# A fourth seven-product pair in every second gate and up group, and the sums of a paired slab one piece earlier

## The chip, the core and the metric

The kernel runs on one core of a Trainium2 chip. The metric is the device time of one execution in microseconds (us). The core has a matrix engine (TensorE, PE in the profile, with its weight loads shown apart as PEld), a vector engine (VectorE, DVE), a scalar engine (ScalarE, ACT), GpSimd (POOL) and SyncE (SP). In this kernel SP and POOL mostly issue DMA transfers, each from its own queue and in order.

## The reference: one layer of a hybrid encoder

256 rows of width 2048 go through an input projection into four mixers (gated linear attention, a Fourier mixer, long convolutions, a short convolution), an output projection, cross attention over 256 memory rows, and a gated feed-forward block, with a norm ahead of each and one at the end. Everything is fp32. The part that the change touches is the first half of the feed-forward block:

```
def swiglu(h, w_gate_up, w_down):
    gate, up = jnp.split(h @ w_gate_up, 2, axis=-1)
    return (jax.nn.silu(gate) * up) @ w_down
```

Here h is 256 x 2048, w_gate_up is 2048 x 11264 (5632 gate columns, then 5632 up columns) and w_down is 5632 x 2048.

## The kernel before

**Precision.** Every fp32 weight tile is split into a high part (a cast by ScalarE, `wh`) and the rest (a subtraction by VectorE, `wl`). Activations are kept split in the same way. One product of a 128 x 128 activation tile with a 128 x 512 weight tile is then three matmuls, in `part` (lines 433 to 435): high by `wh`, high by `wl`, low by `wh`. All three add into one PSUM bank.

**Slabs.** All weights are laid out in one array, in the order of use, as slabs of 128 x 2048 (four tiles of 128 x 512). `Stream` loads slabs (`_load`) into three `raw` buffers and splits them piece by piece into pairs `wh` and `wl`. There are four such pairs in these stages (three in one pool, a fourth in `extra`), used in turn, and `_fill` keeps at most four pieces in being: the one in use and three ahead. A plain slab (N in a plan) has two pieces of 1024 columns; it serves 8 products, 24 matmuls.

**Paired slabs.** For two k tiles, two column groups (512 gate columns and the 512 up columns that go with them) and the two halves of the 256 rows, eight products can be had from seven, if sums of weight tiles and sums of activation tiles are formed first. A paired slab (S in a plan) holds the four weight tiles and serves 7 products, 21 matmuls. The activation sums `z` are formed once by `combine`, before the first paired group. The weight sums are formed for each slab, in `_sums`, which makes four pieces of 1024, 512, 1024 and 1024 columns. They feed 2, 1, 2 and 2 products.

Weight sums come in two ways. For a slab in `SUMMED` (all paired slabs of gate and up) SP loads three of the four tiles, and two sums are made by a transfer: SP loads one tile twice into `two`, and a POOL transfer adds two others onto it (lines 99 to 103). VectorE then needs two additions. For the others (all paired slabs of the down projection) the whole slab is loaded and VectorE makes four additions, each of 512 columns. In both cases the additions are issued with the third piece (line 157), ahead of its cast (159) and subtraction (160).

**Groups.** Gate and up have 11 column groups. The first uses plain slabs only (`gemm_rows`). Each of the ten others is one call of `paired_rows` with the plan `GROUP`, eight slabs. After its last paired slab ScalarE and VectorE combine the sums (`mixed`, then `gated`); after its last slab `upped` finishes the gated product, VectorE transposes it and POOL stores it to DRAM (`store_turned`). POOL later loads it back, turned, and ScalarE and VectorE split it into the slots `f` of the down projection; this runs in the background.

**Order.** Each engine runs its instructions in the order in which they stand in the built program. That order comes from the order of the calls here and from a scheduler, which moves instructions by its own estimate. Background work (`Background`) is let in when a running count of VectorE work owed, `bg.dve(...)`, is small.

Of the kernel before, what the change touches and what calls it, by code (L numbers as in the profile page):

```python
# [13 lines left out]
F32 = mybir.dt.float32  # L14
F32R = mybir.dt.float32r
# [4 lines left out]
ALU = mybir.AluOpType  # L20
# [3 lines left out]
P = 128  # L24
# [3 lines left out]
DFF = 5632  # L28
# [13 lines left out]
LATE = 12  # L42

GATE_UP = 1920 // 16 + 8
GROUP = "NNSNSNSN"

DOWN = GATE_UP + 80
PASSES = "NNNNSNNSNNSNNSNNSNNSNN", "NSNSNSNSNSNSNSNSNSNNNN"

PAIRED = {a + i for a, plan in [(GATE_UP + 8 * j, GROUP) for j in range(10)] + [(DOWN, PASSES[0]), (DOWN + 22, PASSES[1])]  # L50
          for i, x in enumerate(plan) if x == "S"}
SUMMED = {i for i in PAIRED if i < DOWN}

LAG, OWED, SOON, FAR = 1.3, 0.9, 0.01, 18.0
V_NG = 0
# [16 lines left out]
class Stream:  # L72
# [21 lines left out]
    def _load(self, n):  # L94

        nc = self.nc
        self.raw = self.rawp.tile([P, 2048], F32, name="raw", tag="raw")
        if n // 16 + 1 in SUMMED:
            W, t = self.W[n // 16 + 1], self.sums.tile([P, 1024], F32, name="two", tag="two")
# [12 lines left out]
    def _half(self):  # L112

        nc, n = self.nc, self.made
        if n % 16 == 0 and self.phase == 0:
            self._load(n)
        if n // 16 in PAIRED:
            return self._sums()
# [21 lines left out]
    def _sums(self):  # L140

        nc, r, ph = self.nc, self.raw, self.phase
        summed = self.made // 16 in SUMMED
        if summed:
            src = (r[:, 512:1536], r[:, 0:512], self.two and self.two[0], r[:, 0:1024])[ph]
        else:
            src = (r[:, 512:1536], r[:, 0:512], r[:, 1024:2048], r[:, 0:1024])[ph]
        wh, wl = self._buffers(self.made, src.shape[1])
        if ph == 2:
            s = [r[:, i * 512:i * 512 + 512] for i in range(4)]  # L150
            if summed:
                t = self.two.pop(0)
                ops = ((s[1], t[:, 0:512], s[2]), (s[0], s[1], s[0]))
            else:
                ops = ((s[2], s[2], s[3]), (s[3], s[1], s[3]), (s[1], s[1], s[2]), (s[0], s[0], s[1]))
            for out, a, b in ops:
                nc.vector.tensor_tensor(out=out, in0=a, in1=b, op=ALU.add)  # L157
            self.bg.dve(512 * len(ops), len(ops))
        nc.scalar.copy(wh, src)  # L159
        nc.vector.tensor_tensor(out=wl, in0=src, in1=wh.bitcast(F32), op=ALU.subtract)  # L160
        self.bg.dve(src.shape[1])
        self.halves.append((wh, wl))
        self.phase = (ph + 1) % 4
        if ph == 3:
            self.made += 16
# [27 lines left out]
    def take_sums(self, w, ks, cols):  # L193

        assert self.n // 16 in PAIRED and self.n % 16 == 0
        self.order += [(w, ks[k], cols[c] + i * P) for k, c in ((1, 0), (0, 0), (1, 1), (0, 1)) for i in range(4)]
# [8 lines left out]
class Background:  # L205
# [17 lines left out]
    def first(self, g):  # L223

        self.q.sort(key=lambda e: e[0] is not g)
# [29 lines left out]
class Block:  # L255
# [208 lines left out]
    def paired_rows(self, w, cols, slots, sums, plan, mixed, first, ready=None, late=0, before=None, swap=False):  # L464

        st, s, nk = self.st, len(sums), len(slots)  # L470
        rest = [k for k in range(nk) if not any(k in ks for ks, _ in sums)]
        steps = [(c, k) for c in range(2) for k in rest]
        todo, q = iter(sums), {}
        count = {"a0": len(rest) + s, "a1": len(rest) + s, "b0": len(rest) + s, "b1": len(rest)}
        left, total = {}, 0

        def put(name, hi, lo, wh, wl):
            if name not in q:
                for x in [name] if name in count else "1675":
                    q[x] = (self.bank if (name in count) == swap else self.gbank)()  # L480
                    left[x] = count.get(x, s)
            new = left[name] == count.get(name, s)
            left[name] -= 1
            self.part(q[name][:, :], hi, lo, wh, wl, new, left[name] == 0)

        form = lambda t, r: (t[:, r * P:(r + 1) * P], t[:, R + r * P:R + (r + 1) * P])
        n = done = 0
        for i, kind in enumerate(plan):
            if before:
                before(i)  # L490
            if kind == "S":
                ks, z = next(todo)
                a = [form(slots[ks[0]], 0), form(slots[ks[1]], 0), form(slots[ks[1]], 1)]
                hi, lo, x4 = self.forms(z, slots[ks[0]])
                x1, s2, s3 = ((hi[:, i * P:i * P + P], lo[:, i * P:i * P + P]) for i in range(3))
                t = (("5", x1), ("7", s3))
                pairs = iter((("1", a[0]), ("b0", x4), ("a0", a[1]), *(t if st.n // 16 in SUMMED else t[::-1]), ("a1", a[2]), ("6", s2)))
                for parts in st.take_sums(w, ks, cols):
                    for wh, wl in parts:
                        name, (hi, lo) = next(pairs)  # L500
                        put(name, hi, lo, wh, wl)
                        self.bg.poll()
                done += 1
                if done == s:
                    mixed(*(q[i] for i in "1567"))
            else:
                for c, k in steps[n:n + 4]:
                    if ready:
                        ready(k)
                    wh, wl = st.take(w, k, cols[c], 4)  # L510
                    for r in range(2):
                        put("ab"[c] + str(r), *form(slots[k], r), wh, wl)
                        self.bg.poll()
                n += 4
            if first and done == s and n >= len(rest):
# [531 lines left out]
    def gate_up(self, gp, f, z):  # L1047

        nc = self.nc
# [7 lines left out]
        def up(j, ps, h=None):  # L1057
            h = h or [gp.tile([P, 512], F32, name="h", tag="h", bufs=2) for _ in range(2)]
            for r in range(2):
                self.stt(h[r], ps[r], box["col"][:, r:r + 1], g[r], ALU.mult, ALU.mult)  # L1060
                self.store_turned(self.ff, 4 * j, r, g[r], h[r])
            stored.append(self.bg.now)
# [16 lines left out]
        def upped(j, ps):  # L1079

            for r in range(2):
                self.tt(h[r], h[r], ps[r], ALU.add)
            up(j, h, h)
# [34 lines left out]
        def combined():  # L1118
            for ks, z in sums:
                yield 3.0  # L1120
                yield from self.combine(z, *(self.h3[k] for k in ks))

        sums = [((2 * i, 2 * i + 1), z[i]) for i in range(GROUP.count("S"))]
        comb = self.bg.add(combined())
        ps = self.gemm_rows("w_gate_up", [0, DFF], self.h3,
                            parts=[(range(8), [0]), (range(8, 12), [0]), (range(12), [1]), (range(12, 16), [0]), (range(12, 16), [1])],
# [4 lines left out]
        early = self.bg.add(fetch(0, FT - 22, 3, 2.0, 15))  # L1131
        self.bg.drain(comb)
        for j in range(1, DFF // 512):
            upped(j, self.paired_rows("w_gate_up", [j * 512, DFF + j * 512], self.h3, sums, GROUP, mixed, gated, swap=j % 2 == 0)[0])
        self.bg.drain(early)
        self.fetch = self.bg.add(fetch(FT - 22, FT, 6, SOON))

# [753 lines left out]
```

## Time and profile before

| | |
|---|---|
| median of 3 runs | 1437.34 us (1435.31, 1437.34 and one of 2798.02) |
| the profiled execution | 1435.07 us, of which the span of its instructions is 1433.3 us |
| PE busy | 1423.0 us, 99% of the span |
| VectorE busy | 1146.2 us, 80% |
| ScalarE busy | 815.2 us, 57% |
| the ten paired groups of gate and up | one each 41.48 us; the last runs to about 1193 us |
| DMA engines busy in one such group | 92 to 94%, 287 to 289 GB/s |

A page of the profile shows the busy time of each engine, then the span in 40 slices, the DMA queues, the chain of work that ended last, and the costliest groups of instructions. The time line gives start and duration of single instructions (or of a few equal ones, merged with their count), and in brackets how long the engine was idle before and what ended that. PE busy has one trap: a matmul is shown from its start to its modelled end, 0.39 us, while the next one starts 0.23 us after it. So the busy time of PE only says that no gap was left between matmuls.

### The profile page before, as it was taken

How to read it: one execution, taken by the hardware profiler on the slowest of the kernel's cores; microseconds unless marked ns; L12 is line 12 of the kernel's file. 1: busy time of each engine (PE TensorE's matmuls, PEld its weight loads, DVE VectorE, ACT ScalarE, POOL GpSimd, SP SyncE). 2: the span in 40 equal slices, each digit the busy share in tenths (PEclk: the TensorE clock that was granted, in tenths of full speed). 3: DMA queues.
4: the chain of work that ended last, by engine and by line, in shares of the span. 5: the costliest groups of instructions: out<-in, count | busy, mean ns of one | idle time of the engine just before them, and what ended most of it. 6: DMA issues, size and time to landing. Idle time of an engine off the chain costs nothing.

```text
span 1433.3 us, 18652 instructions
## 1 busy us (share of the span) xinstructions
PE 1423.0 (99%) x6589; PEld 1180.7 (82%) x6589; DVE 1146.2 (80%) x1738; ACT 815.2 (57%) x1183; POOL 234.8 (16%) x306
## 2 busy tenths in 40 slices
PE   9999999999999999999999999999999999999997
PEld 8888888888888888888888888888888888888886
DVE  6667868777877767777677888898888888989997
ACT  7556565446645555556554656555555556655655
POOL 0000100013212223531431121122011002000000
PEclk9999999999999999999999999999999999999999
DMA  9876564546667788964986999889999887655554
GB/s 352 299 285 248 205 206 162 175 169 224 202 196 236 234 267 252 274 200 166 289 239 209 286 286 277 278 275 282 294 293 288 268 260 229 219 230 179 193 218 147
DMA packets 73037, 343.79 MB, mean 240 GB/s; under 512 B 10957, under 2 KB 12654, under 8 KB 45168
## 3 DMA queue, kind: packets, MB, share of 16 engines
q1 hardware_dynamic: 54848, 288.98, 57.5%
q0 software_dynamic: 17664, 52.97, 15.8%
q8 instruction: 51, 0.84, 0.2%
q10 hardware_dynamic: 432, 0.66, 0.1%
q14 instruction: 42, 0.34, 0.1%
HBM read 322.12 MB, written 20.45 MB: 239 GB/s over the span
## 4 chain that ended last, share of the span: by engine, by line
PE 97%; DVE 1%; ACT 0%; DMA 0%; issue 0%; SPq 0%; ACTq 0%
PE pg L433 22%; PE pg L434 22%; PE pg L435 22%; PE pm L434 7%; PE pm L435 7%; PE pm L433 7%; PE pg L381 4%; PE pg L382 2%; PE pm L1344 1%; PE pm L1022 1%; PE pm L993 1%; DMA raw<-in_W 0%; PE pm L1753 0%; DVE res L283 0%; PE pm L994 0%
## 5 line engine op out<-in xcount | busy, mean ns | idle before, releaser
L136 DVE TENSOR_TENSOR wl<-raw,wh 128x1024 fp32r<-128x1024 f32 (+1 forms) x413 | 494.8, 1212 | 166.1 <-ACT wh L135 163.2
L135 ACT CAST wh<-raw 128x1024 fp32r<-128x1024 f32 (+1 forms) x413 | 424.5, 1043 | 283.9 <-PE pg L435 196.4
L433 PE MATMUL pg<-wh,act 128*128 128x512 f32 (+1 forms) x1191 | 465.6, 391 | 0.0
L434 PE MATMUL pg<-wl,act 128*128 128x512 f32 (+1 forms) x1191 | 463.9, 389 | 0.4 <-DVE wl L136 0.2
L435 PE MATMUL pg<-wh,act 128*128 128x512 f32 (+1 forms) x1191 | 463.9, 389 | 0.0
L433 PEld LDWEIGHTS pg<-wh,act 128*128 128x128 f32 x1191 | 223.8, 188 | 47.8 <-issue 1.5
L434 PEld LDWEIGHTS pg<-wl,act 128*128 128x128 f32 x1191 | 223.8, 188 | 47.2 <-DVE wl L136 1.3
L435 PEld LDWEIGHTS pg<-wh,act 128*128 128x128 f32 x1191 | 223.7, 188 | 47.2 <-DVE act L283 0.4
L159 ACT CAST wh<-raw 128x1024 fp32r<-128x1024 f32 (+1 forms) x150 | 137.0, 921 | 146.8 <-DVE raw L157 46.4
L160 DVE TENSOR_TENSOR wl<-raw,wh 128x1024 fp32r<-128x1024 f32 (+1 forms) x150 | 156.1, 1061 | 57.0 <-ACT wh L159 56.8
L434 PE MATMUL pm<-wl,act 128*128 128x512 f32 x309 | 120.5, 390 | 0.1
L433 PE MATMUL pm<-wh,act 128*128 128x512 f32 x309 | 120.2, 389 | 0.0
L435 PE MATMUL pm<-wh,act 128*128 128x512 f32 x309 | 120.2, 389 | 0.0
L381 PE MATMUL pg<-act,wh 128*128 128x512 f32 x256 | 90.5, 395 | 0.0
L382 PE MATMUL pg<-act,wl 128*128 128x256 f32 x256 | 71.8, 280 | 0.0
L434 PEld LDWEIGHTS pm<-wl,act 128*128 128x128 f32 x309 | 58.0, 188 | 13.0 <-DVE wl L136 0.6
L433 PEld LDWEIGHTS pm<-wh,act 128*128 128x128 f32 x309 | 58.0, 188 | 12.0
L435 PEld LDWEIGHTS pm<-wh,act 128*128 128x128 f32 x309 | 58.0, 188 | 12.0
L102 POOL DMA_DIRECT2D two<-in_W x30 | 26.6, 887 | 241.2 <-DMA two<-in_W 116.0
L157 DVE TENSOR_TENSOR raw<-raw 128x512 f32<-128x512 f32 x90 | 62.0, 689 | 1.3
L159 ACT CAST wh<-two 128x1024 fp32r<-128x1024 f32 x30 | 31.6, 1052 | 51.1 <-PE pg L435 21.7
L381 PEld LDWEIGHTS pg<-act,wh 128*128 128x128 f32 x256 | 48.1, 188 | 10.5
(375 smaller groups left out, 1821.9 us busy)
## 6 DMA issues: line engine op xcount, KB each, us to landing
raw<-in_W SPq DMA_DIRECT2D x216, 1024.0 KB, 5.6
raw<-in_W SPq DMA_DIRECT2D x30, 768.0 KB, 6.1
two<-in_W SPq DMA_DIRECT2D x60, 256.0 KB, 4.9
two<-in_W POOLq DMA_DIRECT2D x30, 512.0 KB, 9.3
raw<-in_W SPq DMA_DIRECT2D x11, 512.0 KB, 7.6
hidden<-g POOLq DMA_DIRECT2D x22, 256.0 KB, 3.7
tmp<-hidden POOLq DMA_DIRECT2D x44, 128.0 KB, 5.4
features<-tmp POOLq DMA_DIRECT2D x32, 128.0 KB, 5.3
```

The source lines that it names most:

```text
L102: nc.gpsimd.dma_start(t, W[:, 512:1536], accum_op=ALU.add)
L135: nc.scalar.copy(wh[:, a:b], r[:, a:b])
L136: nc.vector.tensor_tensor(out=wl[:, a:b], in0=r[:, a:b], in1=wh[:, a:b].bitcast(F32), op=ALU.subtract)
L157: nc.vector.tensor_tensor(out=out, in0=a, in1=b, op=ALU.add)
L159: nc.scalar.copy(wh, src)
L160: nc.vector.tensor_tensor(out=wl, in0=src, in1=wh.bitcast(F32), op=ALU.subtract)
L381: self.nc.tensor.matmul(p[:, :], wh, slot[:, :], start=start, stop=False)
L382: self.nc.tensor.matmul(p[:, 0:R], wl, slot[:, 0:R], start=False, stop=stop)
L433: self.nc.tensor.matmul(p, hi, wh, start=start, stop=False)
L434: self.nc.tensor.matmul(p, hi, wl, start=False, stop=False)
L435: self.nc.tensor.matmul(p, lo, wh, start=False, stop=stop)
L993: nc.tensor.matmul(p[:, :], q[d][:, r * P:(r + 1) * P], kt[d][:, :], start=d == 0, stop=False)
```

## The change

There are two edits.

**The sums move.** In `_sums` the additions are issued after the cast and subtraction of the second piece (`ph == 1`), no longer ahead of the third piece. For a summed slab the second addition now writes tile 2 instead of tile 0, so that the fourth piece is `r[:, 512:1536]` instead of `r[:, 0:1024]`; the last two products of such a slab swap places in `paired_rows`. Number and shape of the instructions of a slab stay the same.

**A fourth pair.** Groups 2, 4, 6, 8 and 10 get the plan `NSNSsNSN` instead of `NNSNSNSN`. Their slabs at places 1, 3 and 6 are summed slabs. The slab at place 4, marked s, is a paired slab that isn't in `SUMMED`: it is loaded whole, and VectorE makes its four sums. One more `z` tile holds the activation sums of the fourth pair of k tiles.

```diff
-GROUP = "NNSNSNSN"
+GROUPS = "NNSNSNSN", "NSNSsNSN"
...
-SUMMED = {i for i in PAIRED if i < DOWN}
+SUMMED = {GATE_UP + 8 * j + i for j in range(10) for i, x in enumerate(GROUPS[j % len(GROUPS)]) if x == "S"}
...
-        if summed:
-            src = (r[:, 512:1536], r[:, 0:512], self.two and self.two[0], r[:, 0:1024])[ph]
-        else:
-            src = (r[:, 512:1536], r[:, 0:512], r[:, 1024:2048], r[:, 0:1024])[ph]
+        t = self.two and self.two[0]
+        src = (r[:, 512:1536], r[:, 0:512], t if summed else r[:, 1024:2048], r[:, 512:1536] if summed else r[:, 0:1024])[ph]
         wh, wl = self._buffers(self.made, src.shape[1])
-        if ph == 2:
+        nc.scalar.copy(wh, src)
+        nc.vector.tensor_tensor(out=wl, in0=src, in1=wh.bitcast(F32), op=ALU.subtract)
+        self.bg.dve(src.shape[1])
+        self.halves.append((wh, wl))
+        if ph == 1:
             s = [r[:, i * 512:i * 512 + 512] for i in range(4)]
             if summed:
-                t = self.two.pop(0)
-                ops = ((s[1], t[:, 0:512], s[2]), (s[0], s[1], s[0]))
+                ops = ((s[1], t[:, 0:512], s[2]), (s[2], s[1], s[0]))
             else:
                 ops = ((s[2], s[2], s[3]), (s[3], s[1], s[3]), (s[1], s[1], s[2]), (s[0], s[0], s[1]))
             for out, a, b in ops:
                 nc.vector.tensor_tensor(out=out, in0=a, in1=b, op=ALU.add)
             self.bg.dve(512 * len(ops), len(ops))
-        nc.scalar.copy(wh, src)
-        nc.vector.tensor_tensor(out=wl, in0=src, in1=wh.bitcast(F32), op=ALU.subtract)
-        self.bg.dve(src.shape[1])
-        self.halves.append((wh, wl))
...
-            if kind == "S":
+            if kind in "Ss":
...
-                t = (("5", x1), ("7", s3))
-                pairs = iter((("1", a[0]), ("b0", x4), ("a0", a[1]), *(t if st.n // 16 in SUMMED else t[::-1]), ("a1", a[2]), ("6", s2)))
+                t, u = (("5", x1), ("7", s3)), (("6", s2), ("a1", a[2]))
+                back = slice(None, None, 1 if st.n // 16 in SUMMED else -1)
+                pairs = iter((("1", a[0]), ("b0", x4), ("a0", a[1]), *t[back], *u[back]))
...
-        sums = [((2 * i, 2 * i + 1), z[i]) for i in range(GROUP.count("S"))]
+        z = z + [gp.tile([P, 1024], F32R, name="z3")]
+        sums = [((2 * i, 2 * i + 1), z[i]) for i in range(4)]
...
-            upped(j, self.paired_rows("w_gate_up", [j * 512, DFF + j * 512], self.h3, sums, GROUP, mixed, gated, swap=j % 2 == 0)[0])
+            plan = GROUPS[(j - 1) % len(GROUPS)]
+            upped(j, self.paired_rows("w_gate_up", [j * 512, DFF + j * 512], self.h3, sums[:8 - plan.count("N")], plan, mixed, gated,
+                                      swap=j % 2 == 0)[0])
```

More of the change, by code (lines that the diff above doesn't have):

```diff
@@ L44 @@
 GATE_UP = 1920 // 16 + 8
-GROUP = "NNSNSNSN"
+GROUPS = "NNSNSNSN", "NSNSsNSN"
 DOWN = GATE_UP + 80
 PASSES = "NNNNSNNSNNSNNSNNSNNSNN", "NSNSNSNSNSNSNSNSNSNNNN"
-PAIRED = {a + i for a, plan in [(GATE_UP + 8 * j, GROUP) for j in range(10)] + [(DOWN, PASSES[0]), (DOWN + 22, PASSES[1])]
-          for i, x in enumerate(plan) if x == "S"}
-SUMMED = {i for i in PAIRED if i < DOWN}
+PAIRED = {a + i for a, plan in [(GATE_UP + 8 * j, GROUPS[j % len(GROUPS)]) for j in range(10)] + [(DOWN, PASSES[0]), (DOWN + 22, PASSES[1])]
+          for i, x in enumerate(plan) if x in "Ss"}
+SUMMED = {GATE_UP + 8 * j + i for j in range(10) for i, x in enumerate(GROUPS[j % len(GROUPS)]) if x == "S"}
 LAG, OWED, SOON, FAR = 1.3, 0.9, 0.01, 18.0
@@ L158, in _sums @@
             self.bg.dve(512 * len(ops), len(ops))
-        nc.scalar.copy(wh, src)
-        nc.vector.tensor_tensor(out=wl, in0=src, in1=wh.bitcast(F32), op=ALU.subtract)
-        self.bg.dve(src.shape[1])
-        self.halves.append((wh, wl))
+        if ph == 2 and summed:
+            self.two.pop(0)
         self.phase = (ph + 1) % 4
```

## The prediction

> **What bounds the kernel now.** I read the page's head and the chain of work that ended last, then busy time by stretch, then the waits, then the time line of one gate and up group.
>
> ```profile
> span 1433.3 us, 18652 instructions
> PE 97%; DVE 1%; ACT 0%; DMA 0%; issue 0%; SPq 0%; ACTq 0%
> ```
>
> ```profile
> 820.00:1235.00 415.00, 414.94 (x1829) 342.46 (x1828) 363.44 (x451) 236.92 (x288) 73.11 (x85) 1.00 0.89 274
> 1235.00:1400.00 165.00, 164.97 (x727) 135.83 (x726) 154.06 (x229) 96.25 (x127) 0.00 (x0) 1.00 0.55 203
> ...
> 944.10:985.58 41.48, 41.48 (x185) 34.35 (x183) 36.45 (x45) 24.19 (x30) 7.74 (x9) 1.00 0.92 289
> ...
> 1400.00:1433.00 33.00, 24.54 (x108) 19.55 (x106) 23.85 (x50) 15.86 (x29) 0.00 (x0) 0.94 0.45 159
> ```
>
> The columns are the stretch, its length, then busy time of PE, PEld, DVE, ACT and POOL, the granted clock, DMA share and GB/s. The chain is PE for 97%, and PE has no gap worth a name in gate and up (0.06 us in 415) or in the down projection (0.03 in 165). So time can be won only by taking matmuls away, and lost by any wait that reaches PE. The third row is one whole group: DVE works 36.45 of 41.48 us. It isn't far behind, so the waits need a look (all of 840 to 1200 us; total, times, longest):
>
> ```profile
> DVE wl L160 <- ACT wh L159: 41.7, 41, 1.7
> ACT wh L159 <- PE pm L435: 39.5, 28, 2.1
> ...
> PEld pm L434 <- DVE wl L160: 0.5, 1, 0.5
> ```
>
> PE's side waits once, for 0.5 us. ScalarE waits for PE, that is, for one of the four `wh`/`wl` pairs to come free: the supply is ahead by all that the pairs hold, and no more. How much that is in time depends on the slab.
>
> ```profile
> 933.90 0.39 PE L433 MATMUL pg<-wh,act 128*128 128x512 f32 x1
> ...
> 938.66 0.39 PE L433 MATMUL pm<-wh,act 128*128 128x512 f32 x1
> ...
> 944.10 0.39 PE L433 MATMUL pg<-wh,act 128*128 128x512 f32 x1
> ...
> 985.58 0.39 PE L433 MATMUL pm<-wh,act 128*128 128x512 f32 x1
> ```
>
> These are the starts of a paired slab (place 6), of the plain slab behind it, of the next group and of the one after. A paired slab takes 4.76 us for seven products, 0.68 each; a plain one 5.44 for eight. A plain piece therefore lasts PE 2.72 us, a paired piece 1.36, 0.68, 1.36 and 1.36. Over paired slabs the same four pairs hold half the time.
>
> **The change part by part.** *Matmuls.* Five groups swap a plain slab for a paired one: 5 products, 15 matmuls; the built program has 15 fewer. At 0.68 us each that is **-3.40 us**, certain, since PE has no gaps.
>
> *The fourth z.* Eight more small VectorE operations, once, of at most 0.42 us (row below), 3.4 us in all, and two casts. They fall into the first group, of plain slabs alone, where a slab asks 2.3 us of VectorE in 5.44. Cost nothing; without that cover 3.4 us.
>
> *The sums moved.* Down-projection slabs keep all their VectorE work; only small background operations change sides with the additions. PE waits 0.03 us there, so nothing can be gained; the pieces are ahead by more than the one or two background operations (0.42 us each) that change sides. I take 0, bounds 0 and +1 us.
>
> *Splits of the hidden tiles.* In the built order none of these stands in a changed group; those between hold four or five, and the last four stand together ahead of the down projection, whose first four slabs are plain. Cost 0.
>
> ```profile
> L283 DVE TENSOR_TENSOR f<-tmp,f 128x256 fp32r<-128x256 f32 x14 | 5.9, 419 | 0.0
> ```
>
> *The changed group.* I write T for time since the group's first matmul (944.10 in the trace). These rows carry the rest:
>
> ```profile
> 936.66 3.50 DVE L136 TENSOR_TENSOR wl<-raw,wh 128x1024 fp32r<-128x1024 f32 x3 [0.21 <-ACT wh L135]
> ...
> 944.66 1.22 DVE L136 TENSOR_TENSOR wl<-raw,wh 128x1024 fp32r<-128x1024 f32 x1 [0.38 <-ACT wh L135]
> 945.80 0.68 DVE L283 TENSOR_TENSOR g<-g,pm 128x512 f32<-128x512 f32 x1
> 946.40 1.28 DVE L283 TENSOR_TENSOR h<-h,pm 128x512 f32<-128x512 f32 x2
> 947.60 1.41 DVE L287 SCALAR_TENSOR_TENSOR h<-h,rc,g 128x512 f32<-128x512 f32 x2
> 948.92 1.30 DVE L557 STREAM_TRANSPOSE g<-h 128x512 f32<-128x512 f32 x2
> 950.14 1.18 DVE L136 TENSOR_TENSOR wl<-raw,wh 128x1024 fp32r<-128x1024 f32 x1
> 951.25 1.82 DVE L160 TENSOR_TENSOR wl<-raw,wh 128x1024 fp32r<-128x1024 f32 x2
> ...
> 955.05 0.69 DVE L157 TENSOR_TENSOR raw<-raw 128x512 f32<-128x512 f32 x1
> ```
>
> ```profile
> 1372.88 2.87 DVE L157 TENSOR_TENSOR raw<-raw 128x512 f32<-128x512 f32 x4
> 1375.66 1.22 DVE L160 TENSOR_TENSOR wl<-raw,wh 128x1024 fp32r<-128x1024 f32 x1
> ```
>
> ```profile
> 934.14 1.05 ACT L159 CAST wh<-raw 128x1024 fp32r<-128x1024 f32 x1 [1.71 <-PE pm L435]
> ...
> 1374.40 1.05 ACT L159 CAST wh<-raw 128x1024 fp32r<-128x1024 f32 x1 [2.64 <-DVE raw L157]
> ```
>
> A subtraction of 1024 columns takes 1.22 us and the next operation starts 1.14 after it (three in 3.50); one of 512 takes 0.69 and 0.60. Four additions hold VectorE 2.78 us (1372.88 to 1375.66), and a cast that needs two of them starts 1.52 us after the first (1374.40). A cast takes 1.05 and starts 0.24 us after PE frees its pair (933.90, where the plain slab ends, to 934.14). PE needs `wl` 0.23 us into a product. VectorE's work for the group: 36.45 less two plain subtractions (2.28), plus three of 1024, one of 512 and four additions (3.42 + 0.60 + 2.78) is 41.0 us, less 1.4 for four splits that go elsewhere: 39.6 of PE's 40.80. The mean just fits. The places where it doesn't are two.
>
> *Place 1.* From 944.66 (T+0.56) to 950.14 (T+6.04) VectorE does one subtraction and then the end of the last group. In the built order that subtraction is now the first piece of the paired slab; its second piece, the sums and the rest stand behind the block. VectorE's order there, in groups 4 and 8 of the changed program (its line 148 is the paired slab's subtraction, 158 its additions, 136 a plain slab's):
>
> ```
> L148 wl<-raw 1024     first piece, ahead of the block
> L282 g<-g  L282 h<-h x2  L286 h<-h x2  L557 g<-h x2
> L148 wl<-raw 512      second piece
> L158 raw<-two
> L148 wl<-two 1024     third piece
> L158 raw<-raw
> L136 wl<-raw 1024     slab behind, first piece
> L148 wl<-raw 1024     fourth piece
> ```
>
> In groups 2, 6 and 10 both pieces of the slab behind stand ahead of the fourth piece. PE used to have two plain slabs, 10.88 us, ahead of the first paired one; now it has 5.44.
> - VectorE: second piece T+6.04, done 6.73; addition at 6.64; third piece 7.24 to **8.46**; addition to 9.07; then, as built, one or two plain subtractions of the slab behind (8.99 to 10.21, or to 11.35), and the fourth piece to **11.48** or **12.49**.
> - PE: pieces begin at T+5.44, 6.80, 7.48. The third piece's `wl` is needed at 7.71: a wait of 0.75. It ends at 9.59; the fourth's `wl` is needed at 9.82: a wait of 1.66 where one plain subtraction stands ahead (groups 4 and 8), 2.67 where two do (2, 6, 10).
>
> Together 2.41 or 3.42 us. The lower bound is 0 (the order on the chip finds slack that I don't see), the upper 3.42 in all five groups.
>
> *Place 4, the slab s.* Its pieces follow those of a paired slab, whose pairs come free late in short steps. With t for PE's start on the paired slab at place 3: first pair free t+1.36, cast 1.60 to 2.65, subtractions 2.68 and 3.82, additions 4.42 to 7.29, third piece 7.20 to **8.42**. PE wants it at 4.76 + 2.04 + 0.23 = 7.03: a wait of 1.39, and that piece ends at 9.55. In the built order a plain subtraction stands ahead of the fourth piece as well: 8.34, then 9.48 to **10.70**, wanted at 9.78: 0.92. Together **2.31 us**. In the down projection the same additions hurt no one, since a plain slab (5.44 us) stands ahead of each such slab. Lower bound 0, if background order spares it; the upper bound comes with the load of the slab:
>
> ```profile
> raw<-in_W SPq DMA_DIRECT2D x38, 1024.0 KB, 7.5
> ```
>
> ```profile
> DMA to landing us min/median/max: 5.8/7.3/9.7
> ```
>
> SP can issue it when place 1's fourth piece is done (T+11.5 or 12.5), so it lands at about T+19.0 or 20.0, and its first cast is due at T+19.65 or 20.66. A load of 9.7 us would come 1.6 us late. I take 0; upper bound 1.6 in each of five groups. The added summed slabs' transfers (SP's, then POOL's) keep four slabs or more between the release of `two` and its next use, as now, and POOL's order has three of them per group as before: 0.
>
> *Sum.* Groups 4 and 8: 2.41 + 2.31 = 4.72; groups 2, 6 and 10: 5.73. Waits 2 x 4.72 + 3 x 5.73 = 26.6, less 3.4: **+23.2 us**. The profiled execution took 1435.07 us (its span and 1.8 around it), 2.3 below the median of the runs; from it 1458.3, and I say **1458 us**, 1.6% up. About 2% is what a measurement of this kernel can tell from no change.
>
> The Trainium skill (Perfetto Trace Analysis, Identifying the Most-Contended Engine) says that kernels generally improve when the most-contended engine is relieved; that is PE here, and by that rule the change gives the first rival's time. The 36.45 of 41.48 us that VectorE already works in a group, with a whole piece of lead lost at place 1, speaks against it.
>
> **The rivals.**
> - *Not slower: the four pairs cover it.* VectorE's mean work stays below PE's time, and the trace shows a lead of all four pairs almost always. If the third piece at place 1 is ready 0.75 us sooner and the slab s finds its first pairs 1.4 us sooner, no wait reaches PE: 1435.07 - 3.4 = **1431.7 us**. Against it: the block from 944.66 to 950.14 is fixed by PE's group end, and pairs aren't free before PE is done with them.
> - *Late load of s.* All five loads take 9.7 us: 5 x 1.6 = 8 more, **1466 us**, just over 2%. For it: DMA is busy 92% in a group; against it: the median leaves 0.65 us.
> - *The clock falls in the new gaps.* In the last 33 us PE stands 8.46 us idle and the clock is 0.94: 2.0 us lost, 0.23 for each idle us. On 26.6 us of gaps that is 6.3 more: **1465 us**. Against it: those end gaps are longer than mine, the longest of which is 2.67 us. The Trainium skill (TensorE: Matmul & The Clock Gate, HAM oscillation) puts the danger at idle gaps above about 3.4 us; by that rule the clock stays at 1.00 here. No run shown so far has such gaps in mid-kernel.
> - *It isn't done as said.* The built program has the four additions in five slabs and 15 matmuls fewer, so no.
>
> **How the numbers follow.** Forecast, waits at both places, 1444 to 1464: 0.68. Waits at one place alone or half as long, 1435 to 1444: 0.08. Not slower, about 1432: 0.08. Late loads, the clock, or waits that add up differently, 1464 to 1480: 0.16. The range 1438 to 1470 leaves out the not-slower rival, part of the half case and the far end of the last: near 0.2. Slower by over 2% (above about 1465): 0.17; faster by over 2%: 0.01, as no more than 3.4 us can be won; within: 0.82.
>
> **What would show it.** In the changed profile PE's idle time in the ten groups should be about 27 us, all in the five changed ones, ended by VectorE's `wl` of paired slabs; changed groups should last 45.5 and 46.5 us and the others 41.48 as now. At place 1 two gaps of 0.75 and 1.7 or 2.7 us, at place 4 of 1.4 and 0.9. Granted clock 1.00 and the down projection without gaps. The prediction is wrong if changed groups last 40.8 us, if their gaps end with a DMA, or if the other groups grow.

## The result, and the profile after

The changed kernel takes **1456.74 us** (median of four runs, 1456.05 to 1457.85), the kernel before 1437.09 on the same chip (median of four, one of which took 2798.02 us and is left out of the ratio): a ratio of **1.014 [1.0127, 1.0153]**, 1.4% slower. The forecast was 1458 us. The profiled execution took 1456.53 us (before: 1435.07), its span grew from 1433.3 to 1454.8, by 21.5 us.

The page's head, the busy time of each engine and the chain that ended last, of the kernel after:

```profile
span 1454.8 us, 18657 instructions
...
PE 1432.8 (98%) x6574; PEld 1176.6 (81%) x6574; DVE 1169.7 (80%) x1776; ACT 823.2 (57%) x1195; POOL 235.1 (16%) x306
...
PE 81%; DVE 9%; DMA 6%; ACT 2%; issue 2%; SPq 0%; ACTq 0%; DVEq 0%
```

VectorE's busy share is 80% as before; PE's share of the chain fell from 97 to 81%, VectorE's rose from 1 to 9, and that of the DMA, all of it loads of raw slabs, from 0 to 6. So the average didn't move, the order of what ends last did.

To see where, the span is cut at the first copy of each group's combining (`mixed`), which comes once per group. Busy time by stretch, kernel after: length, then PE, PEld, DVE, ACT, POOL, granted clock, DMA share, GB/s. These are groups 2, 3, 6 and 7:

```profile
810.15:857.01 46.86, 44.35 (x182) 34.59 (x181) 39.69 (x46) 24.34 (x29) 7.73 (x9) 0.96 0.88 260
857.01:898.45 41.44, 41.44 (x184) 34.26 (x183) 35.78 (x43) 24.28 (x30) 7.79 (x9) 1.00 0.89 273
985.59:1029.70 44.11, 42.55 (x181) 33.11 (x180) 39.99 (x48) 24.56 (x29) 6.06 (x7) 1.00 0.88 261
1029.70:1071.41 41.71, 41.71 (x185) 34.49 (x184) 36.02 (x43) 23.72 (x29) 6.06 (x7) 1.00 0.88 276
```

The full list is 46.86, 41.44, 45.28, 41.86, 44.11, 41.71, 43.89, 41.64 and 44.51 us; before, nine times about 41.48. A changed group without any wait would take 40.80 (41.48 less 0.68), so the five lose 6.1, 4.5, 3.3, 3.1 and 3.7 us, 20.7 in all; the groups between lose next to nothing. The first copy stands at 810.15 (before 810.17). From the last copy to the end it is 253.35 us, before 249.22: 4.1 more. So 20.7 in the changed groups, less 3.4 for the matmuls that went, plus 4.1 in the down projection, is 21.4 of the span's 21.5.

What PE waited for over the ten groups of the kernel after (total, times, longest):

```profile
PE pg L432 <- ACT wh L147: 4.6, 8, 1.0
PE pg L433 <- DVE wl L148: 4.0, 7, 0.7
PE pm L432 <- ACT wh L135: 0.9, 4, 0.2
```

Lines 147 and 148 are the cast and the subtraction of a paired slab. This view counts only idle time after a modelled end (0.39 us), so it shows less than is lost; from the starts of the matmuls, taken 0.23 us apart, the five groups lose 1.6, 2.1, 1.3, 2.1 and 1.9 us at **place 1** (9.1) and 2.4, 2.0, 1.9, 0.8 and 1.8 at **place 4** (9.0). Another 1.6 us of group 2 are a fallen clock (below). About 1 us of the 20.7 is in none of these sums.

Place 1 in group 6, VectorE's time line after:

```profile
1000.50 0.65 DVE L148 TENSOR_TENSOR wl<-raw,wh 128x512 fp32r<-128x512 f32 x1
1001.07 0.68 DVE L158 TENSOR_TENSOR raw<-two,raw 128x512 f32<-128x512 f32 x1
1001.66 1.22 DVE L148 TENSOR_TENSOR wl<-two,wh 128x1024 fp32r<-128x1024 f32 x1
1002.80 0.68 DVE L158 TENSOR_TENSOR raw<-raw 128x512 f32<-128x512 f32 x1
1003.40 2.35 DVE L136 TENSOR_TENSOR wl<-raw,wh 128x1024 fp32r<-128x1024 f32 x2
1005.67 2.35 DVE L148 TENSOR_TENSOR wl<-raw,wh 128x1024 fp32r<-128x1024 f32 x2
```

The second piece, an addition, the third piece, an addition, two plain pieces, the fourth piece: VectorE runs without a break behind the block of the last group, as the prediction wrote it down, and the fourth piece's `wl` is done at 1006.89. PE in the same stretch:

```profile
1002.43 0.50 PE L432 MATMUL pm<-wh,act 128*128 128x512 f32 x1
1002.93 0.50 PE L433 MATMUL pg<-wl,z 128*128 128x512 f32 x1
...
1004.62 0.49 PE L432 MATMUL pg<-wh,z 128*128 128x512 f32 x1 [0.48 <-ACT wh L147]
1004.95 0.39 PE L432 MATMUL pm<-wh,act 128*128 128x512 f32 x1
1005.18 0.40 PE L433 MATMUL pm<-wl,act 128*128 128x512 f32 x1
...
1007.26 0.39 PE L433 MATMUL pg<-wl,z 128*128 128x512 f32 x1
```

From 1004.95 to 1007.0 PE does three whole products of the plain slab *behind*, whose `wl` was done early, and only at 1007.26 turns to the fourth piece's `wl`. The gap is 0.65 us, where 2.67 were forecast, and it isn't a wait for `wl`. It ends with ScalarE's cast of the fourth piece, which starts when VectorE's second addition is done (1003.48):

```profile
1003.51 2.00 ACT L147 CAST wh<-raw 128x1024 fp32r<-128x1024 f32 x2 [0.19 <-DVE raw L158]
```

Place 4, the slab s. ScalarE's first two casts of s in groups 2, 4, 6 and 10, then that of its third piece in group 10:

```profile
839.30 1.57 ACT L147 CAST wh<-raw 128x1024 fp32r<-128x1024 f32 x2 [1.52 <-DMA raw<-in_W]
...
928.01 1.57 ACT L147 CAST wh<-raw 128x1024 fp32r<-128x1024 f32 x2 [1.30 <-DMA raw<-in_W]
...
1013.12 1.57 ACT L147 CAST wh<-raw 128x1024 fp32r<-128x1024 f32 x2 [0.54 <-DMA raw<-in_W]
...
1184.87 1.57 ACT L147 CAST wh<-raw 128x1024 fp32r<-128x1024 f32 x2 [0.35 <-PE pm L434]
1189.21 1.05 ACT L147 CAST wh<-raw 128x1024 fp32r<-128x1024 f32 x1 [2.78 <-DVE raw L158]
```

VectorE in group 10, the first two pieces of s, the additions and the third piece:

```profile
1185.95 1.83 DVE L148 TENSOR_TENSOR wl<-raw,wh 128x1024 fp32r<-128x1024 f32 x2 [0.18 <-ACT wh L147]
1187.69 2.86 DVE L158 TENSOR_TENSOR raw<-raw 128x512 f32<-128x512 f32 x4
1190.47 1.22 DVE L148 TENSOR_TENSOR wl<-raw,wh 128x1024 fp32r<-128x1024 f32 x1
```

So what comes last here is a chain: a pair or the load, a cast, two subtractions, the additions, the cast of the third piece, PE. In groups 8 and 10 the chain starts when PE frees a pair, as the prediction has it; in groups 2, 4 and 6 it starts with the load of s, 1.17, 1.17 and 0.18 us after the time at which the pair would have let the cast begin (in groups 8 and 10 it begins 0.47 us after the start of the last matmul that uses the pair). VectorE has pauses here: in group 10 it stops four times between 1180 and 1186, for 1.5 us in all, each time for a cast.

### The profile page after: what moved, and what is told of

Read it like the earlier page. It is cut to its first block, busy times and chain, and to the rows that moved or that the text cites. A ratio compares the mean times of both kernels' runs of the same rounds, so it can differ in the third digit from the quotient of the medians.

```text
span 1454.8 us, 18657 instructions
## 1 busy us (share of the span) xinstructions
PE 1432.8 (98%) x6574; PEld 1176.6 (81%) x6574; DVE 1169.7 (80%) x1776; ACT 823.2 (57%) x1195; POOL 235.1 (16%) x306
## 4 chain that ended last, share of the span: by engine, by line
PE 81%; DVE 9%; DMA 6%; ACT 2%; issue 2%; SPq 0%; ACTq 0%; DVEq 0%
PE pg L433 19%; PE pg L434 19%; PE pg L432 19%; DMA raw<-in_W 6%; PE pm L432 4%; PE pm L433 4%; PE pm L434 4%; PE pg L380 4%; DVE wl L136 3%; PE pg L381 2%; DVE wl L148 2%; DVE raw L158 1%; ACT wh L135 1%; PE pm L1347 1%; ACT wh L147 1%
## 5 line engine op out<-in xcount | busy, mean ns | idle before, releaser
L136 DVE TENSOR_TENSOR wl<-raw,wh 128x1024 fp32r<-128x1024 f32 (+1 forms) x403 | 483.3, 1212 | 164.2 <-ACT wh L135 161.9
L135 ACT CAST wh<-raw 128x1024 fp32r<-128x1024 f32 (+1 forms) x403 | 414.9, 1042 | 278.1 <-PE pg L434 192.6
L147 ACT CAST wh<-raw 128x1024 fp32r<-128x1024 f32 (+1 forms) x170 | 155.7, 922 | 169.3 <-PE pg L434 59.7
L148 DVE TENSOR_TENSOR wl<-raw,wh 128x1024 fp32r<-128x1024 f32 (+1 forms) x170 | 177.4, 1061 | 49.6 <-ACT wh L147 49.1
L432 PE MATMUL pm<-wh,act 128*128 128x512 f32 x279 | 109.4, 395 | 1.0 <-ACT wh L135 0.9
L433 PE MATMUL pm<-wl,act 128*128 128x512 f32 x279 | 109.6, 393 | 0.3 <-DVE wl L136 0.2
L434 PE MATMUL pm<-wh,act 128*128 128x512 f32 x279 | 108.9, 390 | 0.0
L158 DVE TENSOR_TENSOR raw<-raw 128x512 f32<-128x512 f32 x110 | 75.5, 687 | 1.6
L432 PEld LDWEIGHTS pm<-wh,act 128*128 128x128 f32 x279 | 52.5, 189 | 14.6 <-ACT wh L135 3.9
L433 PEld LDWEIGHTS pm<-wl,act 128*128 128x128 f32 x279 | 52.5, 188 | 13.8 <-DVE wl L148 1.7
L434 PEld LDWEIGHTS pm<-wh,act 128*128 128x128 f32 x279 | 52.5, 188 | 10.7
```

The costliest lines, as they stand in the source:

```text
L135: nc.scalar.copy(wh[:, a:b], r[:, a:b])
L136: nc.vector.tensor_tensor(out=wl[:, a:b], in0=r[:, a:b], in1=wh[:, a:b].bitcast(F32), op=ALU.subtract)
L432: self.nc.tensor.matmul(p, hi, wh, start=start, stop=False)
L433: self.nc.tensor.matmul(p, hi, wl, start=False, stop=False)
L434: self.nc.tensor.matmul(p, lo, wh, start=False, stop=stop)
```

## The experiments

Every kernel is the changed kernel with the edit shown. Periods are the stretches between first copies, as above; groups 2, 4, 6, 8 and 10 are the first, third, fifth, seventh and ninth.

### Each part alone

**The moved sums without the fourth pair.**

```diff
-GROUPS = "NNSNSNSN", "NSNSsNSN"
+GROUPS = "NNSNSNSN", "NNSNSNSN"
```

> The moved sums alone, all ten groups with the old plan. Theory A (the four weight pairs give too short a lead at places 1 and 4 of the changed groups, and the background work that they push back costs some 4 us at the start of the down projection): 1435 to 1438 us, no gap of PE in gate and up, none above 0.6 us at the start of the down projection. Rival B (the moved additions hold VectorE at the wrong moment, in either stage): 1445 us or more, or at least the 4 us at the start of the down projection.

Measured: 1436.74 us, 1.0002 [0.9993, 1.0012]; periods 41.5 to 41.7 but for the last (42.9), the last stretch 249.38. The busy time by stretch of this kernel, to be set beside the same stretch of before:

```profile
820.00:1235.00 415.00, 414.16 (x1822) 341.16 (x1821) 362.46 (x449) 236.53 (x287) 73.09 (x85) 1.00 0.89 273
```

PE is idle 0.84 us in 415, nearly all of it in the last period. The medians agree within the interval, so the move is worth nothing that these runs can tell.

**The fourth pair with the sums at the third piece, as they were.**

```diff
-        nc.scalar.copy(wh, src)
-        nc.vector.tensor_tensor(out=wl, in0=src, in1=wh.bitcast(F32), op=ALU.subtract)
...
-        if ph == 1:
+        if ph == 2:
...
                 nc.vector.tensor_tensor(out=out, in0=a, in1=b, op=ALU.add)
             self.bg.dve(512 * len(ops), len(ops))
+        nc.scalar.copy(wh, src)
+        nc.vector.tensor_tensor(out=wl, in0=src, in1=wh.bitcast(F32), op=ALU.subtract)
```

> The fourth pair alone, sums issued with the third piece as before. Theory A: 1454 to 1460 us, with gaps at the same two places and some 4 us at the start of the down projection. Rival B: 1434 to 1440 us. If the move helps the slab s at all, this one is slower than 1457 by some us.

Measured: 1456.38 us, 1.014 [1.0125, 1.0156], the same as the whole change. The fourth pair carries all of the loss; earlier sums neither caused it nor soften it. Its parts lie a little otherwise: the first copy 1.7 us later, the last stretch 250.91.

**A paired slab at place 1 alone**, three paired slabs, all summed by transfers:

```diff
+GROUPS = "NNSNSNSN", "NSNNSNSN"
```

> Changed groups with the plan NSNNSNSN: three summed pairs as before, only the first of them at place 1 in place of place 2; as many matmuls as before. Theory A: gaps of 1.3 to 2.3 us at place 1 in five groups as in the changed kernel, so some 9 us: 1443 to 1447 us. Rival C (only the slab s is at fault, by its four additions or its load): 1435 to 1438 us.

Measured: 1443.12 us, 1.0044 [1.0029, 1.0059]. The changed groups last 43.63, 42.86, 42.58, 42.60 and 42.59 against 41.48 (there are three paired slabs again, so no matmuls are saved): 6.9 us.

**The slab s behind a paired one alone**, with two plain slabs ahead, three paired slabs:

```diff
+GROUPS = "NNSNSNSN", "NNSsNNSN"
```

> Changed groups with the plan NNSsNNSN: three pairs, the second of them an s right behind the first; as many matmuls as before, place 1 plain. Theory A: gaps of 1.3 to 4.3 us behind the paired slab in five groups as in the changed kernel, some 12 us without place 1: 1445 to 1450 us. If place 1 were the only cause: 1435 to 1438 us.

Measured: 1442.64 us, 1.0043 [1.0026, 1.006], less than expected. The changed groups last 43.32, 42.83, 43.27, 43.33 and 42.74: 8.1 us over 41.48, and all gaps stand at the slab s. PE's waits in the groups of this kernel:

```profile
PE pg L432 <- ACT wh L147: 2.3, 5, 0.7
PE pm L432 <- ACT wh L135: 1.2, 5, 0.3
```

PE is held first by the cast of the slab's third piece, which waits for the additions. So the two places cost 13.5 us over before when each is alone (7.0 and 6.5 over the 1436.12 us that before took on that chip). The whole change loses 19.7, or 23.1 with its 3.4 us of saved matmuls: 9.6 come only with both together, of which 4.1 are the down projection and 1.6 the clock; the rest are longer waits at the two places (the slab s stands at place 3 here and at place 4 in the changed kernel, so the comparison is rough).

**The changed plan in groups 1, 3, 5, 7 and 9.** The two plans trade places:

```diff
+GROUPS = "NSNSsNSN", "NNSNSNSN"
```

> The changed plan in groups 1, 3, 5, 7 and 9 in place of 2, 4, 6, 8 and 10, so that a group of the old plan stands ahead of the down projection. Theory A (the changed kernel's 4.1 us in the down projection come from background work pushed back by the last groups): the down projection takes what it took before, and the whole 1451 to 1455 us. If that cost has another cause: 1456 to 1459 us.

Measured: 1455.75 us, 1.0126 [1.0108, 1.0144]; now the second, fourth, sixth and eighth periods are the long ones (44.75, 47.03, 46.01, 44.82) and the others are 41.3 to 42.2. The loss goes with the plan, not with where a group stands. The total lies between the two ranges: with a group of the old plan ahead of it, the last stretch falls by 2 us, to 251.3, and not to the 249.2 of before.

### Is it the pairs, or VectorE?

The prediction explained place 4 by pairs that come free late. A fifth pair should take that away; a kernel without the additions takes VectorE's work away.

**A fifth pair, with the plan NNSsNNSN, first with narrower pairs.** To make room the pairs became 1072 columns wide instead of 1088 (only 1024 are used).

```diff
+GROUPS = "NNSNSNSN", "NNSsNNSN"
...
-        return (pool.tile([P, 1088], F32R, name=t, tag=t)[:, at:at + m] for t in ("wh", "wl"))
+        return (pool.tile([P, 1072], F32R, name=t, tag=t)[:, at:at + m] for t in ("wh", "wl"))
...
+            pool = (self.wp, self.wp, self.wp, self.extra, self.fifth)[(i - self.h0) % 5]
```

> The plan NNSsNNSN of the run with s behind a paired slab (1442.6 us), with a fifth weight pair in use during the paired groups and so one piece more of lead (the four small tiles that it takes the room of come from the common pool). Theory A: the gaps behind the paired slab vanish or fall under 0.5 us: 1434 to 1438 us. If it is VectorE's throughput or the load of s that lacks and not the lead: 1441 us or more.

Measured: 1465.66 us, 1.0204 [1.0183, 1.0224]. It doesn't answer the question, since 13 us were lost *ahead* of the first paired group (first copy 823.45 instead of 810.2). The same holds for two runs with the same width, in which all four paired slabs were summed by transfers:

```diff
+GROUPS = "NNSNSNSN", "NSNSSNSN"
-tc.tile_pool(name="tw", bufs=2)
+tc.tile_pool(name="tw", bufs=3)
```

> The changed groups' slab s made a summed slab too (plan NSNSSNSN): two additions by VectorE in place of four, two more of its sums by a POOL transfer, with a third buffer for these. Theory A: the wait behind the paired slab falls from 1.3 to 4.3 us to under 1 us in five groups, that of place 1 stays: 1446 to 1452 us. Rival C (transfers late): no faster than the changed kernel, or gaps that end with a DMA.

```diff
+GROUPS = "NNSNSNSN", "NNSSNSSN"
-tc.tile_pool(name="tw", bufs=2)
+tc.tile_pool(name="tw", bufs=3)
```

> Changed groups with the plan NNSSNSSN, all four pairs summed, a third buffer for the sums: two plain slabs first, so no paired slab at place 1, and two additions in place of four behind a paired slab. As many matmuls as the changed kernel. Theory A: gaps under 1 us a group, and with 3.4 us of matmuls less 1432 to 1440 us. Rival C: each of these groups loads 0.75 MB more, and 1445 us or more with gaps that end with a DMA.

Measured: 1482.73 us, 1.0314 [1.0288, 1.034], and 1482.95 us, 1.0314 [1.0287, 1.0342], with first copies at 823.99 and 823.37. Two of the three were run again at 1088 columns.

**The fifth pair, pairs 1088 wide.** The edit is shown against the kernel with the narrower pairs.

```diff
-tile([P, 1072], F32R, name=t, tag=t)
+tile([P, 1088], F32R, name=t, tag=t)
```

> The plan NNSsNNSN of e4_behind in every second group, with a fifth wh/wl pair during gate and up, and the pairs as wide as in the kernel before (1088 columns; e7_five had 1072). Theory A (the paired slab behind a paired slab stalls PE because four pairs are too little lead for it): the changed groups fall from 43 us to 41.5 or less, 1434 to 1438. If it is the load of the slab or VectorE's throughput that limits, the changed groups stay at 42.5 or more, at least 1441. If the 1072 columns alone made e7_five slow, its 13 us ahead of the first paired group and its 6 us in the down projection are gone here.

Measured: 1448.98 us (1444.98 to 1449.24; the profiled execution is the shortest), 1.0075 [1.0059, 1.0092]; the first copy is back at 810.27, the last stretch at 250.83. The changed groups last 44.03, 42.60, 44.17, 42.29 and 42.95: no better than with four pairs (43.32, 42.83, 43.27, 43.33, 42.74). So in this plan the pairs are not what the slab s lacks. VectorE's time line of this kernel behind the end of group 5 (here 155 is a paired slab's subtraction, 165 its additions, 143 a plain one's):

```profile
995.37 1.78 DVE L155 TENSOR_TENSOR wl<-raw,wh 128x1024 fp32r<-128x1024 f32 x2
997.07 0.68 DVE L165 TENSOR_TENSOR raw<-two,raw 128x512 f32<-128x512 f32 x1
997.68 1.22 DVE L155 TENSOR_TENSOR wl<-two,wh 128x1024 fp32r<-128x1024 f32 x1
998.81 0.68 DVE L165 TENSOR_TENSOR raw<-raw 128x512 f32<-128x512 f32 x1
1000.69 1.23 DVE L155 TENSOR_TENSOR wl<-raw,wh 128x1024 fp32r<-128x1024 f32 x1 [1.19 <-ACT wh L154]
1001.83 0.42 DVE L295 TENSOR_TENSOR f<-tmp,f 128x256 fp32r<-128x256 f32 x1
1002.17 1.82 DVE L155 TENSOR_TENSOR wl<-raw,wh 128x1024 fp32r<-128x1024 f32 x2
1003.90 2.86 DVE L165 TENSOR_TENSOR raw<-raw 128x512 f32<-128x512 f32 x4
1006.68 1.22 DVE L155 TENSOR_TENSOR wl<-raw,wh 128x1024 fp32r<-128x1024 f32 x1
```

From the end of the group's block (995.4) to the third piece of s (done 1007.90) VectorE stops once, for 1.19 us, in which ScalarE casts what VectorE has just added. With a pair free, the next piece is still behind VectorE's own queue.

That holds for this plan only. With four pairs and the same plan ScalarE didn't wait for a pair at s in any of the five groups: its last cast of the slab ahead waited 1.7 to 2.6 us for that slab's additions, and the first cast of s followed at once. A fifth pair had nothing to take away there. In the changed kernel the pair does come last in groups 8 and 10, and no run gave that plan a fifth pair. The median here is 6 us above that of the four pairs (1442.64); the runs don't tell why.

**The changed kernel without the four additions.**

```diff
-            for out, a, b in ops:
+            for out, a, b in ops if summed or self.made // 16 >= DOWN else ():
```

> The changed kernel without the four additions of the slab s in gate and up (its sums are left out, so its products use unsummed weight tiles); everything else as in the changed kernel, the running count of VectorE work too. Theory V (VectorE has no slack in the 25 us behind a group's end, and the additions, 2.78 us in each of five groups, are what it lacks): the gaps behind the first paired slab, 12.6 us in the changed kernel, go, those at place 1 (9.4 us) stay or shrink; the changed groups fall to 41.5 to 43.5 us, total 1441 to 1447. Theory P (short pieces that free their pairs late, or the late load of s): more than half of those gaps stays, at least 1450. The down projection should stay at about +4 in both.

Measured: 1447.26 us, 1.0073 [1.0055, 1.0092], 9.5 below the changed kernel and 0.3 above the upper end of what theory V expected. Group 6 of this kernel, with 37.41 us of VectorE's work where the changed kernel has 39.99:

```profile
981.15:1023.18 42.03, 41.48 (x180) 33.31 (x179) 37.41 (x44) 24.38 (x30) 6.06 (x7) 1.00 0.92 276
```

From the starts of PE's matmuls, 0.3 us of gaps are left at place 4 in all five groups together; those at place 1 stay (1.4 us in group 6, changed kernel 1.3), and so does the down projection's loss (last stretch 253.6). The nine periods sum to 380.6 instead of 391.3: 10.7 less, which is the 9.0 us of place 4 and the 1.6 of the clock; 1.5 us are lost anew ahead of the first copy. 2.78 us of additions in each group cost up to 2.4 us of PE's time there, and without them place 4 loses nothing of note. The run doesn't show that the late pair or the late load plays no part beside them: the prediction's own chain, with t for PE's start on the slab ahead and shorter by 2.78 us, has the third piece done at t+5.64, ahead of the t+7.03 at which PE wants it. In group 6 of this kernel the first cast of s, held by a pair, comes even later than in the changed kernel (t+2.29), and PE doesn't wait.

### All four slabs summed by transfers

If VectorE is short, its additions can be given to transfers. Plan NNSSNSSN, a third `two` buffer, pairs 1088 wide (and, as with the fifth pair, four small tiles taken from the common pool to make room):

```diff
+GROUPS = "NNSNSNSN", "NNSSNSSN"
-tc.tile_pool(name="tw", bufs=2)
+tc.tile_pool(name="tw", bufs=3)
```

> Every second group NNSSNSSN: four paired slabs, all summed by transfers, a third buffer for them, two plain slabs first, pairs 1088 wide. Theory A: the changed groups last 41 to 42 us as in e6_nnss. The question is whether the other groups, plan as before, stay at 41.5 (then about 1433 to 1436, no slower than before) or lose 3 to 6 us each to the added transfers, as they did with 1072 columns (then 1450 to 1465).

Measured: 1468.23 us, 1.0216 [1.0196, 1.0237]. The stretches of groups 3, 4 and 5 of this kernel; group 4 has the new plan:

```profile
857.99:904.03 46.04, 42.95 (x188) 34.60 (x187) 37.86 (x46) 24.79 (x31) 8.61 (x10) 1.00 0.92 287
904.03:944.47 40.44, 40.44 (x178) 32.86 (x177) 37.66 (x47) 23.64 (x30) 7.74 (x9) 1.00 0.91 271
944.47:992.42 47.95, 44.70 (x186) 35.18 (x185) 37.76 (x46) 24.58 (x30) 8.59 (x10) 0.96 0.92 282
```

The groups with four paired slabs take 41.17, 40.44, 42.82, 40.71 and 41.70, near the 40.80 of no wait. The groups *between*, whose plan is untouched, take 46.04, 47.95, 47.93 and 46.30. The total is above the upper range. Over the nine periods ScalarE's casts of plain slabs wait 44.1 us for loads of raw slabs, up to 7.7 at a time; in the kernel before it was 15.7, up to 4.3. What the new groups gained was paid back in the next ones. Another 6.6 us are lost ahead of the first copy (816.82), and 2.5 in the last stretch. Which queue or engine sets that price was not taken apart.

### The down projection

**The changed kernel, with the additions of s left out of the running count.**

```diff
-            self.bg.dve(512 * len(ops), len(ops))
+            if summed or self.made // 16 >= DOWN:
+                self.bg.dve(512 * len(ops), len(ops))
```

> The changed kernel, but the four additions of slab s in gate and up are left out of the running count of VectorE work owed, so that the splits of the hidden tiles are let in earlier, in the changed groups too. Theory A (the 4.1 us in the down projection come from the last of these splits, which are pushed back in front of it): the stretch from the last combined group to the end falls from 253.35 us to 249 to 251, total 1452 to 1455. If the 4.1 us have another cause, that stretch stays at 252.5 or more.

Measured: 1457.59 us, 1.0145 [1.0128, 1.0162]. The last stretch falls to 249.94 us as expected, but the total doesn't fall, which was not: the nine periods sum to 393.5 instead of 391.3 us, and the first copy comes 0.5 later. In the changed kernel four splits of the hidden tiles, ten being done by then, are left for the start of the down projection:

```profile
1216.03 1.39 DVE L282 TENSOR_TENSOR f<-tmp,f 128x256 fp32r<-128x256 f32 x4
1217.33 4.62 DVE L136 TENSOR_TENSOR wl<-raw,wh 128x1024 fp32r<-128x1024 f32 x4
1221.87 0.42 DVE L282 TENSOR_TENSOR z<-tmp,z 128x256 fp32r<-128x256 f32 x1
```

```profile
1232.97 0.50 PE L434 MATMUL pg<-wh,z 128*128 128x512 f32 x1 [1.34 <-DVE z L282]
...
1240.56 0.50 PE L433 MATMUL pg<-wl,act 128*128 128x512 f32 x1 [0.53 <-DVE wl L136]
```

The first fence is VectorE, the second PE: the four splits stand ahead of four plain pieces, the activation sums `z` of the down projection come behind those, and PE loses 1.49 us there by its starts and 1.03, 0.81 and 0.75 us at three later places, together 4.1. In this experiment all 14 splits are done before the last copy, and the first two of these waits are gone; the last two stay (0.7 and 0.6 us), so the splits aren't their cause, which stays open. Of the 3.4 us that the last stretch wins, 2.2 return in the groups, the span is only 0.7 us shorter, and the median not at all. In these groups the splits aren't free either.

## Why the prediction was right, and where it was not

The total came within 1.3 us (1458 against 1456.74), but not all terms did.

- *Matmuls, -3.4*: right. The traces hold 6589 and 6574 matmuls, 15 fewer, and PE had no gaps before.
- *The fourth z, 0*: right. The first copy stands at 810.15, before at 810.17.
- *The sums moved, 0*: right, by the run of that part alone, 1.0002.
- *Place 1, 2.41 or 3.42 in each group, 15.1 in all*: **9.1**. VectorE's half of the step was right within 0.2 us: in group 6 the third piece was to be done at T+8.46 and the fourth at T+12.49, and they were done at T+8.29 and T+12.30 (T is 994.59, 9.0 us behind the first copy as in the group of before). The half that failed is "PE: pieces begin at T+5.44, 6.80, 7.48": it takes PE piece by piece. The built program has PE's products mixed, several `wh` matmuls and three whole products of the slab behind ahead of the late `wl`, and these cover about 2 us of the second gap (0.65 instead of 1.66 or 2.67; the first, forecast at 0.75, came as 0.59 in group 6). The step used VectorE's own order and left PE's out. It also left out that the fourth piece's cast waits for the second addition; that wait is the 0.65.
- *Place 4, 2.31 in each group, 11.6 in all*: **9.0**. The chain was right. For the first cast, the first subtraction, the additions, the third and the fourth piece's subtraction the prediction has t+1.60, 2.68, 4.42, 7.20 and 9.48; in group 10 (t, PE's start on the slab at place 3, is 1183.26) they started at t+1.61, 2.69, 4.43, 7.21 and 9.48, and in group 8 within 0.02 of the forecast. The wait for the third piece came as 1.34 us in group 10 (forecast 1.39), that for the fourth as 0.45 (forecast 0.92), since products of the slab behind stand between: PE's order again. Group 8 lost only 0.8.
- *The load of s, 0*: too little. In group 2 (T is 819.15) it landed when forecast (839.20, T+20.05), but the pair was ready for the cast at T+18.98 and not at T+20.66, because PE had lost less at place 1 than forecast. So the load came last in three groups, by up to 1.17 us. What it cost PE isn't separated: these groups lost 1.9 to 2.4 us at place 4, the two others 0.8 and 1.8.
- *Splits of the hidden tiles, 0*: **4.1**. The prediction saw that four are left ahead of the down projection and counted its plain slabs as cover. It left out that the sums `z` of the down projection are queued behind these splits on VectorE. With the splits let in earlier, 3.4 of the 4.1 go.
- *Sum*: 20.7 of waits in the groups where 26.6 were forecast, 4.1 where 0 was: 24.8 against 26.6. That the total fits so well is partly luck; the two errors have opposite signs. Of the signs that the prediction named, long changed groups beside others near 41.48 came true; PE's gaps end with a cast of ScalarE (4.6 us) more than with VectorE's `wl` (4.0), and neither the clock nor the down projection stayed untouched.

The rivals. *Not slower* fell: the means fit (39.99 of VectorE's us in a group of 40.80), and still 20.7 us were lost, because VectorE's work bunches behind each group's end at place 1, and at place 4 the additions stand in a chain that can't start before a pair and the load are there. By the Trainium skill (Perfetto Trace Analysis, Identifying the Most-Contended Engine) relieving PE should have gained; here 3.4 us less of PE's work cost 24.8 of waits. The Trainium skill (Perfetto Trace Analysis, Optimization Strategy) says that the most-contended engine can change over time; the chain of this case agrees, with VectorE at 9% of it instead of 1. *Late load* came true in part: in three groups the load was the last to come, though by less than 1.6 us and without the 8 us more in all. *The clock falls* came true once, in group 2, for 1.6 us; in the other four changed groups it stayed at 1.00.

## What to carry to other kernels

An engine whose mean work fits can still be the bound where its work bunches: add up its queue from the end of the last group to the piece that is wanted, not over a whole group. When a wait is sized, read the order of the engine that waits as well as that of the engine it waits for; independent work behind the late piece covers part of it. A test of a cause must run where that cause is at work: the fifth pair was tried on a plan in which no cast at s waited for a pair. Work that a change pushes out of the groups, background work above all, lands somewhere, and what is queued behind it there belongs to the sum.

## What the runs showed of the hardware that was not expected

**The width of the split pairs changes PE's rate.** Two kernels that differ only in whether these tiles are 1072 or 1088 columns wide took 1465.66 and 1448.98 us. The same 100 us, long before any group, in which both do the same work; first the narrower, then the wider:

```profile
100.00:200.00 100.00, 100.00 (x440) 81.33 (x439) 76.23 (x118) 64.81 (x108) 8.73 (x17) 1.00 0.65 224
```

```profile
100.00:200.00 100.00, 100.00 (x450) 82.73 (x449) 76.83 (x118) 64.60 (x108) 8.56 (x16) 1.00 0.65 229
```

PE has no gap and a granted clock of 1.00 in both, and does 440 matmuls instead of 450: from 120 to 160 us the starts stand 0.230 us apart instead of 0.227. The two other kernels with 1072 columns have 0.230 as well, and the kernel before, the changed kernel and the plan NNSSNSSN at 1088 columns 0.227. The width shifts where every tile in the pool, and what is allotted after it, lies in SBUF. Which address does it was not tried.

**The clock can fall after gaps of about 1 us.** In group 2 of the changed kernel, PE's time line:

```profile
844.75 0.73 PE L432 MATMUL pg<-wh,z 128*128 128x512 f32 x2 [0.97 <-ACT wh L147]
846.18 0.50 PE L433 MATMUL pg<-wl,z 128*128 128x512 f32 x1 [0.70 <-DVE wl L148]
...
847.39 0.63 PE L432 MATMUL pm<-wh,act 128*128 128x512 f32 x1
847.82 0.63 PE L432 MATMUL pg<-wh,z 128*128 128x512 f32 x1
```

Behind gaps of 1.1 and 0.9 us eight matmuls last about 0.63 us instead of 0.39 and start 0.42 apart; the granted clock of the stretch is 0.96. With the two plans swapped it happened in one group as well (0.96 there, behind gaps of 0.8 and 1.4 us), with the uncounted additions in one (1.1 and 0.9 us), and with NNSSNSSN at 1088 columns in two (behind gaps of 2.7 and 2.5 us), while the fourth pair with late sums had gaps of the same size in group 2 and stayed at 1.00. The Trainium skill (TensorE: Matmul & The Clock Gate, HAM oscillation) puts the danger at gaps above about 3.4 us; these five groups fell behind shorter ones, so the measurement decides against taking that figure as safe. What makes one such gap harmless and the next not, the runs don't tell.
